# Gate columns of a hybrid decoder layer by Strassen's block product, seven products for eight

## The chip, the cores and the metric

The kernel runs on one core of a Trainium2 chip. The metric is the device time of one execution in microseconds (us). The core has a matrix engine (TensorE, PE in the rows), a vector engine (VectorE, DVE), a scalar engine (ScalarE, ACT), a general engine (GpSimd, POOL) and a queue engine (SyncE, SP), which here issues all transfers between DRAM and the on-chip memory. Each engine works through its own list of instructions in order and waits where an operand or a buffer is not there yet.

## The reference, cut to what matters

```python
h = rms_norm(x, norm_w)                       # x: 2048 tokens x 1024 channels
proj = h @ w_in                               # 8716 columns in all
(u_a, z_a, q, k, v, z_b, xbc, dt, z_c, gate_logits) = split(proj)
y_a = s5_mixer(u_a, ...) * silu(z_a)          # state space branch
y_b = attention_mixer(q, k, v, ...) * silu(z_b)
y_c = ssd_mixer(xbc, dt, z_c, ...)
gates = sigmoid(gate_logits)                  # 3 x 1024 columns: the gate columns
merged = gates_0*(y_a@proj_a) + gates_1*(y_b@proj_b) + gates_2*(y_c@proj_c)
return x + merged @ w_out
```

The change concerns the 3072 columns `gate_logits`, the last part of `h @ w_in`.

## The kernel before, in words

Everything is float32, and each operand of a large product is split in two numbers, hi and lo, that the matrix engine takes at its fast rate (`F32R`). A product is then three passes: hi by hi, hi by lo, lo by hi. The tokens are worked on in two halves of 1024, each of two blocks (`tb`) of 512. `hT[tb]` holds the normed input of a block, transposed: eight channel groups (`kt`) of 128 by 512 tokens, as hi and lo.

For each half the kernel goes through the columns of `w_in`: in the first half `main_qkv`, `main_dtz`, `main_xbc`, `main_uz`, `main_gates`; in the second `main_uz`, `main_qkv`, `main_dtz`, `main_xbc`, `main_gates`. These loops `yield` after each group of output columns (a step), and `run` puts pieces of other work between the steps by a table of step numbers: the attention, the tables and scans of the two state space branches (`s5`, `ssd`), the merge of the attention groups, and `out_weights`, which splits the later projection weights and stores them in DRAM (`pw_d`, `wo_d`). After both halves `final` forms the gated sum and the output projection. The order written there is a priority; the order in each engine's list is then fixed ahead of the run by a scheduler.

`main_gates` takes 12 units of 256 columns per half. For each unit it loads 1 MiB of raw weights (`wr`), ScalarE writes the hi part (`wh`, L368) and VectorE the lo part (`wl`, L369), and `ch_unit` (L392 to L394) forms four outputs of 128 columns by 512 tokens, each of 8 x 3 matmuls. ScalarE applies tanh (`e_g`, L571) and SP stores the result to `g_d`. The second half loads and splits the same weights anew.

A tile pool gives buffers by tag. `ev` has nine buffers of 128x512, shared by nearly everything that leaves an engine; `xb` has three; weights have a pool of their own, `wp`, with one `wr`, six `wh` and six `wl`.

## Time and profile before

| | |
|---|---|
| Time before, median of 3 runs (lowest to highest) | 2508.61 us (2507.28 to 2509.72) |
| The profiled execution, its time | 2515.92 us |
| Its span in the trace | 2513.9 us |
| Busy share of the span: PE, DVE, ACT, POOL | 97%, 53%, 31%, 28% |
| Mean granted clock of TensorE | 0.989 of full |
| Moved by DMA, mean rate | 453.41 MB, 180 GB/s |

The span is the time between the first and the last record of the profiled execution; its own time is 2 us longer, and 7.3 us above the median. Busy shares are sums over the whole span. A matmul's record covers its way through the array, so that records of neighbours overlap: the time that one takes from the next is the distance of their starts.

### The profile page before, as it was taken

To read this page: it belongs to the slowest core of one execution; us is meant where nothing else is said; L and a number is where in the kernel's file an instruction comes from. 1 tells how busy PE (TensorE), PEld (TensorE's weight loads), DVE (VectorE), ACT (ScalarE), POOL (GpSimd) and SP (SyncE) were. 2 spreads that over 40 slices of the span, in tenths; PEclk is the share of its full clock that TensorE was granted. 3 is DMA by queue.
4 is the path that set the end of the run, shared out by engine and by line. 5 is a ranking of instruction groups with operands and counts; after the bars stand their busy time and mean duration, and the time that the engine had idled before them with its cause. 6 is when DMAs were issued, how large, how long until landed. Compare 5 with 4: busy or idle time off the path is not lost.

```text
span 2513.9 us, 40157 instructions
## 1 busy us (share of the span) xinstructions
PE 2450.5 (97%) x15216; PEld 2155.8 (86%) x15216; DVE 1325.0 (53%) x2852; ACT 782.5 (31%) x1656; POOL 700.4 (28%) x737
## 2 busy tenths in 40 slices
PE   8999999999999999999999999999999899999999
PEld 8999988778888888899999988888888678888988
DVE  6963667853544333277765545632334767563321
ACT  4222235443443324222244244533332312121100
POOL 2262243501434430054342000000111455432120
PEclk8999999999999999999999999999999999999999
DMA  6443344447995336455554432433333688887986
GB/s 162 117 147 117 127 134 132 139 135 213 324 340 183 127 100 212 125 160 172 155 171 153 127 107 85 151 122 126 112 126 113 227 294 298 302 293 261 315 291 217
DMA packets 417088, 453.41 MB, mean 180 GB/s; under 512 B 103040, under 2 KB 358272, under 8 KB 409728
## 3 DMA queue, kind: packets, MB, share of 16 engines
q1 hardware_dynamic: 416896, 450.86, 56.2%
q8 instruction: 120, 1.97, 0.3%
q14 instruction: 72, 0.59, 0.1%
HBM read 304.80 MB, written 145.97 MB: 179 GB/s over the span
## 4 chain that ended last, share of the span: by engine, by line
PE 76%; DMA 8%; DVE 8%; POOL 4%; SPq 2%; issue 1%; ACT 1%; DVEq 0%; ACTq 0%; POOLq 0%
PE ps_g L392 6%; PE ps_g L394 6%; PE ps_g L393 6%; PE fp L1299 3%; PE fp L1301 3%; PE fp L1300 3%; PE ao L688 3%; PE ps_xbc L393 2%; PE ps_xbc L394 2%; PE ps_xbc L392 2%; PE ps_uz L394 2%; PE ps_uz L392 2%; PE ps_uz L393 2%; PE op L1332 2%; PE op L1330 2%; PE op L1331 2%
## 5 line engine op out<-in xcount | busy, mean ns | idle before, releaser
L392 PE MATMUL ps_g<-hT_hi,wh_g 128*128 128x512 f32 x768 | 308.4, 402 | 0.6 <-DVE e_uz L466 0.6
L394 PE MATMUL ps_g<-hT_hi,wl_g 128*128 128x512 f32 x768 | 306.4, 399 | 0.0
L393 PE MATMUL ps_g<-hT_lo,wh_g 128*128 128x512 f32 x768 | 305.7, 398 | 0.0
L813 POOL TENSOR_TENSOR sr<-tle,ahl 128x384 fp32r<-128x384 f32 x128 | 119.9, 960 | 447.3 <-PE sd L818 343.2
L392 PEld LDWEIGHTS ps_g<-hT_hi,wh_g 128*128 128x128 f32 x768 | 144.3, 188 | 33.3 <-DVE e_uz L466 1.3
L394 PEld LDWEIGHTS ps_g<-hT_hi,wl_g 128*128 128x128 f32 x768 | 144.5, 188 | 32.8
L393 PEld LDWEIGHTS ps_g<-hT_lo,wh_g 128*128 128x128 f32 x768 | 144.4, 188 | 32.4
L1299 PE MATMUL fp<-fy_hi,fp 128*128 128x512 f32 x384 | 153.9, 401 | 1.8 <-DMA fp<-pw_d 1.3
L1332 PE MATMUL op<-fo,fm_lo 128*128 128x256 f32 x512 | 146.6, 288 | 7.2 <-DVE fm_lo L1312 7.2
L1330 PE MATMUL op<-fo,fm_hi 128*128 128x256 f32 x512 | 148.0, 289 | 4.0 <-DMA fo<-wo_d 2.8
L1301 PE MATMUL fp<-fy_hi,fp 128*128 128x512 f32 x384 | 150.9, 393 | 0.0
L1300 PE MATMUL fp<-fy_lo,fp 128*128 128x512 f32 x384 | 150.3, 391 | 0.0
L1331 PE MATMUL op<-fo,fm_hi 128*128 128x256 f32 x512 | 146.3, 286 | 0.0
L1304 POOL TENSOR_TENSOR fm<-fm,fg 128x512 f32<-128x512 f32 x64 | 85.0, 1328 | 204.4 <-DVE fg L1302 193.7
L667 ACT ACTIVATE sm<-sm,ml 128x256 f32<-128x256 f32 (+1 forms) x192 | 86.4, 451 | 154.4 <-DVE ml L665 127.0
L392 PE MATMUL ps_xbc<-hT_hi,wh_xbc 128*128 128x512 f32 x320 | 129.7, 405 | 0.0
L394 PE MATMUL ps_xbc<-hT_hi,wl_xbc 128*128 128x512 f32 x320 | 129.4, 404 | 0.0
L393 PE MATMUL ps_xbc<-hT_lo,wh_xbc 128*128 128x512 f32 x320 | 129.1, 404 | 0.0
L369 DVE TENSOR_TENSOR wl_g<-wr_g,wh_g 128x512 fp32r<-128x512 f32 x96 | 75.1, 804 | 98.5 <-ACT wh_g L368 93.5
L506 DVE SCALAR_TENSOR_TENSOR ac_cv<-xb_cv,convw,ac_cv 128x512 f32<-128x512 f32 x120 | 101.3, 844 | 38.8 <-ACT ac_cv L504 38.5
L381 PE MATMUL ps_q<-wh_q,hT_hi 128*128 128x256 f32 x384 | 112.2, 293 | 2.1 <-ACT hT_hi L324 1.7
L382 PE MATMUL ps_q<-wl_q,hT_hi 128*128 128x256 f32 x384 | 110.8, 289 | 3.4 <-DVE wl_q L369 3.4
(418 smaller groups left out, 6922.7 us busy)
## 6 DMA issues: line engine op xcount, KB each, us to landing
fp<-pw_d SPq DMA_DIRECT2D x32, 1536.0 KB, 6.9
fo<-wo_d SPq DMA_DIRECT2D x16, 2048.0 KB, 8.7
wr_g<-in_w_in_dram SPq DMA_DIRECT2D x24, 1024.0 KB, 5.4
g_d<-e_g SPq DMA_DIRECT2D x96, 256.0 KB, 2.7
fg<-g_d SPq DMA_DIRECT2D x96, 256.0 KB, 7.4
pw_d<-owh SPq DMA_DIRECT2D x24, 512.0 KB, 7.1
wr_xbc<-in_w_in_dram SPq DMA_DIRECT2D x10, 1024.0 KB, 5.5
x<-in_x_dram SPq DMA_DIRECT2D x32, 256.0 KB, 5.4
```

What stands on the lines that cost most here:

```text
L381: nc.tensor.matmul(ps, hi[:, t], wh, start=kt == 0, stop=False)
L382: nc.tensor.matmul(ps, hi[:, t], wl, start=False, stop=False)
L392: nc.tensor.matmul(ps, wh, hi, start=kt == 0, stop=False)
L393: nc.tensor.matmul(ps, wh, lo, start=False, stop=False)
L394: nc.tensor.matmul(ps, wl, hi, start=False, stop=kt == KT - 1)
L813: nc.gpsimd.tensor_mul(r, self.tle.unsqueeze(1).to_broadcast([P, 3, P]), ahl[:, i, h0:h0 + 3].unsqueeze(2).to_broadcast([P, 3, P]))
L1299: nc.tensor.matmul(ps, W[k][0], yh[k], start=k == k0, stop=False)
L1300: nc.tensor.matmul(ps, W[k][0], yl[k], start=False, stop=False)
L1301: nc.tensor.matmul(ps, W[k][1], yh[k], start=False, stop=k == k1 - 1)
L1330: nc.tensor.matmul(ps, mh[k][:, t], W[k][0], start=k == 0, stop=False)
L1331: nc.tensor.matmul(ps, mh[k][:, t], W[k][1], start=False, stop=False)
L1332: nc.tensor.matmul(ps, mlo[k][:, t], W[k][0], start=False, stop=k == 7)
```

## The change

The gate columns of a unit are now formed as one product of two by two blocks. The rows of the block product are the two token blocks of a half, the inner index is the two halves of the eight channel groups (`kt` 0 to 3 and 4 to 7), and the columns are the two groups of 128 columns of the unit. Eight products of four channel groups (12 matmuls each) become seven, in Winograd's form of Strassen's scheme: four sums of token blocks (S1 to S4) and four of weight blocks (T1 to T4) go in, and the outputs are sums that are partly left in the PSUM bank where the next product adds to them (`x`, `z`, `w` in the code).

The token sums are made once per half by `sums` (S3 and S4 go through DRAM as `sum_d`, and `late_sums` fetches them when the gates begin; S4 then lies where the second block's first four channel groups lay). The weight operands of the seven products are made in the first half by `ops_made` (four raw pieces of 256 KiB, four differences on GpSimd, seven splits), and each is stored as 512 KiB in `gw_d`; in the second half `ops_read` loads the 84 operands from there and nothing is split. Operands go through a ring of five buffers (`sw`) and are asked for three products ahead. A copy of a bank that a later output needs is kept in an `ev` buffer by ScalarE (`keep`), and VectorE adds it to a bank before the tanh.

To make room, buffers move: the weight pool is closed and opened anew at five places (`room_for_sums` before the third unit of `main_uz` in the first half and before `main_xbc` in the second, the start and the end of `main_gates`), `out_weights` works in halves in `ev` buffers, the merge uses `xb` and `ev`, `xb` has four buffers, some buffers of the attention and the scan go from two or three to one or two, and the scan loads its next chunk at the end of a chunk. The attention of the second half is spread over steps 198 to 250 instead of 198 to 256, the scan of the first half starts at step 89 instead of 83, and `out_weights` at 92 instead of 88.

```diff
-ATTEND = 256
+ATTEND = 250
...
+    def room_for_sums(self, half):
+        self.close_left()
+        self.xq = self.left_pool(f"xq{half}")
+        self.wp = self.left_pool(f"wq{half}")
...
+            if half == 0 and u == 2:
+                self.room_for_sums(half)
...
+        if half:
+            self.room_for_sums(half)
...
+    def sums(self, half):
+        nc = self.nc
+        v, gp = nc.vector, nc.gpsimd
+        t0, t1 = self.hT[2 * half], self.hT[2 * half + 1]
+        self.S = {}
+        for i in (1, 2):
+            self.S[i] = tuple(self.xq.tile([P, 4, 512], F32R, name=f"S{i}_{half}_{x}") for x in ("hi", "lo"))
+        for k in range(4):
...
+                gp.tensor_add(a[nm], hi.bitcast(F32), lo.bitcast(F32))
+            s1, s2, s3, s4 = a["22"], self.ev(f"s2_{half}_{k}"), a["21"], a["12"]
...
+            for i, x in ((1, s1), (2, s2)):
+                self.split(x, self.S[i][0][:, k, :], self.S[i][1][:, k, :])
+            yield
+    def split(self, x, hi, lo):
+        self.nc.scalar.copy(hi, x)
+        self.nc.vector.tensor_sub(lo, x, hi.bitcast(F32))
...
+        for i, dst in ((1, t1[0:4]), (0, [tuple(q[:, k, :] for q in q3) for k in range(4)])):
+            for k in range(4):
+                e = self.ev(f"sl{half}_{i}_{k}")
+                nc.sync.dma_start(e, self.sum_d[i, k])
+                self.split(e, *dst[k])
...
+    def op_tile(self, name):
+        return self.wp.tile([P, 2, 4, P], F32R, name=name, tag="sw", bufs=5)
+    def ops_made(self, u):
...
+        for i, j in ((0, 0), (0, 1), (1, 1), (1, 0)):
+            t = self.gp.tile([P, 528], F32, name=f"gr{u}_{i}{j}", tag="xb", bufs=4)
...
+        def diff(i, a, b):
+            t = self.ev(f"gt{u}_{i}", (P, 4, P))
+            nc.gpsimd.tensor_sub(t, a, b)
+            return t
+        def put(p, x):
+            t = self.op_tile(f"gw{u}_{p}")
+            self.split(x, t[:, 0], t[:, 1])
+            nc.sync.dma_start(self.gw_d[u, p - 1], t.bitcast(F32).rearrange("p x k c -> p (x k c)"))
+            return t
+        yield 1, put(1, b11)
+        t1 = diff(1, b12, b11)
+        yield 5, put(5, t1)
...
+        t3 = diff(3, b22, b12)
+        t4 = diff(4, b21, t2)
+        yield 7, put(7, t3)
+        yield 4, put(4, t4)
+    def ops_read(self, u):
+        for p in (1, 5, 6, 3, 2, 7, 4):
+            t = self.op_tile(f"gw{u}_{p}")
+            self.nc.sync.dma_start(t.bitcast(F32).rearrange("p x k c -> p (x k c)"), self.gw_d[u, p - 1])
+            yield p, t
     def main_gates(self, half):
         nc = self.nc
...
+            order += [(u, p) for p in ((1, 5) if u < 11 else (1, 2, 5))]
+            if u:
+                order.append((u - 1, 4))
+            order += [(u, p) for p in ((6, 3, 2, 7) if u < 11 else (6, 3, 7, 4))]
-            wt = self.wtile(f"g{u}_{half}", [(C_G + u * 256, 256)])
...
+        weights(0, 1)
+        weights(0, 5)
+        self.late_sums(half)
+        t0, t1 = self.hT[tb[0]], self.hT[tb[1]]
+        opnd = {1: t0[0:4], 2: t0[4:8], 4: t1[4:8], 5: self.S[1], 6: self.S[2], 7: self.S[3], 3: self.S[4]}
...
+        for n, (u, p) in enumerate(order):
+            w = weights(u, p)
+            for x in order[n + 1:n + 4]:
+                weights(*x)
...
+            ps = bank["z"] if p in (5, 3) else bank["w"] if p == 2 else bank[u, "x"]
+            for k, (hi, lo) in enumerate(opnd[p]):
+                wh, wl = w[:, 0, k, :], w[:, 1, k, :]
+                nc.tensor.matmul(ps, wh, hi, start=k == 0 and p in (1, 2, 5), stop=False, skip_group_check=True)
+                nc.tensor.matmul(ps, wh, lo, start=False, stop=False, skip_group_check=True)
+                nc.tensor.matmul(ps, wl, hi, start=False, stop=k == 3 and p in (2, 3, 4), skip_group_check=True)
...
+            if u == 11 and p == 2:
+                if half:
+                    self.ysplit = [self.load_y(0)]
...
-                ps = self.mmps([P, 512], f"ps_{nm}")
-                self.ch_unit(wt, tb, m, ps)
-                e = self.ev(f"e_{nm}")
-                nc.scalar.activation(e, ps, AF.Tanh, scale=0.5)
...
+            for q in range(2):
+                raw = self.ev(f"ow{j}_{q}")
+                nc.sync.dma_start(raw, src[0, k * P:(k + 1) * P, q * 512:q * 512 + 512])
+                hl = [self.gp.tile([P, 512], F32R, name=f"ow{x}{j}_{q}", tag="ev", bufs=9) for x in "hl"]
...
-        run([(ssd0, 64, 83, 135), (early0, 8, 86, 122), (self.out_weights(), 20, 88, 134)], 136)
+        run([(self.sums(0), 4, 81, 87)], 88)
+        run([(ssd0, 64, 89, 135), (early0, 8, 90, 124), (self.out_weights(), 20, 92, 134)], 136)
```

How the lists of the engines differ, at three places. SP's list while the gates of the first half run: `gr` is a raw weight piece, `gw_d` the stored operands, `ow`, `pw_d`, `wo_d` belong to `out_weights`, `g_d` are results. Before, from the load of one unit's weights on:

```order
L353 DMA wr_g_0_8029<-in_w_in_dram 128x8x256 [waits DMAHW3_49,DVE_49]
L783 DMA sx_8127<-xs_d 128x768 [waits DMAHW4_49,PE_49,Pool_49]
L860 DMA yc_d<-sz_7363 128x6x128 [waits DMAHW5_49,Activation_49]
L1248 DMA wo_d<-owh_9062 128x4x256 [waits DMAHW6_49,Activation_49]
L1248 DMA wo_d<-owh_9062 128x4x256 [waits DMAHW7_49,DVE_49]
L1237 DMA ow_9316<-in_w_out_dram 128x1024 [waits DMAHW0_49]
L1248 DMA wo_d<-owh_9190 128x4x256 [waits DMAHW1_49,Activation_49]
L1248 DMA wo_d<-owh_9190 128x4x256 [waits DMAHW2_49,DVE_49]
L334 DMA hT_d<-xe_0_7727 128x4x128 [waits DMAHW3_49,Activation_49]
```

and after the change, within one unit:

```order
L1433 DMA pw_d<-owl_0_7870 128x4x128 [waits DMAHW4_49,DVE_49]
L649 DMA gw_d<-gw_6_7821 128x1024 [waits DVE_49]
L649 DMA gw_d<-gw_3_7883 128x1024 [waits DMAHW6_49,DVE_49]
L649 DMA gw_d<-gw_2_7902 128x1024 [waits DMAHW7_49,DVE_49]
L1433 DMA pw_d<-owh_1_7877 128x4x128 [waits DMAHW0_49,Activation_49]
L1433 DMA pw_d<-owl_1_7878 128x4x128 [waits DMAHW1_49,DVE_49]
L697 DMA g_d<-g_g_0_7918 128x512 [waits DMAHW2_49,Activation_49]
L638 DMA gr_01_7955<-in_w_in_dram 128x4x128 [waits DMAHW3_49,Pool_49]
L638 DMA gr_11_7957<-in_w_in_dram 128x4x128 [waits DMAHW4_49]
```

Between two results there are now stores of operands (128x1024 is 512 KiB) as well as the transfers of `out_weights`, which went further ahead before.

SP's list at the third unit of `main_uz` in the first half, the load of its raw weights with its neighbours, before:

```order
L469 DMA ua_d<-e_uz_1_0_6429 1024x1x64 [waits DMAHW5_49,Activation_49]
L469 DMA ua_d<-e_uz_0_1_6495 1024x1x64 [waits DMAHW6_49,Activation_49]
L353 DMA wr_uz_0_6890<-in_w_in_dram 128x8x256 [waits DMAHW7_49,DVE_49]
L691 DMA o_d_73<-ob_2_1_6332 128x264 [waits DMAHW0_49,DVE_49]
L1070 DMA p_d<-s5p_6539 128x512 [waits DMAHW1_49,Activation_49]
```

and after:

```order
L490 DMA ua_d<-e_uz_0_1_6861 1024x1x64 [waits Activation_49]
L372 DMA wr_uz_0_6900<-in_w_in_dram 128x8x256 [waits DMAHW3_49,PE_49]
L957 DMA sbt_7689<-bmT_d 128x2x128 [waits DMAHW5_49,DMAHW4_49,PE_49]
L490 DMA ua_d<-e_uz_1_1_6889 1024x1x64 [waits Activation_49]
L959 DMA sct_8100<-cmT_d 128x2x128 [waits DMAHW6_49]
L372 DMA wr_uz_0_7099<-in_w_in_dram 128x8x256 [waits DMAHW7_49,DMAHW3_49,DVE_49]
```

The load waited for VectorE, which reads the same buffer's former content when it splits; now it waits for PE, since the new pool's buffer lies where weights of the unit ahead lay, and it stands behind a result of that unit.

PE's list right there, before:

```order
L393 MATMUL ps_uz_1_1_6862<-hT_1_lo,wh_uz_0_3_6684 128x512
L394 MATMUL ps_uz_1_1_6862<-hT_1_hi,wl_uz_0_3_6685 128x512
L392 MATMUL ps_uz_0_0_6908<-hT_0_hi,wh_uz_0_0_6892 128x512 [waits PE_49]
L393 MATMUL ps_uz_0_0_6908<-hT_0_lo,wh_uz_0_0_6892 128x512
L394 MATMUL ps_uz_0_0_6908<-hT_0_hi,wl_uz_0_0_6893 128x512
L392 MATMUL ps_uz_0_0_6908<-hT_0_hi,wh_uz_0_0_6892 128x512
L393 MATMUL ps_uz_0_0_6908<-hT_0_lo,wh_uz_0_0_6892 128x512
```

and after:

```order
L1001 MATMUL sd_3_7442<-sr_3_0_7438,tgtr 128x384 [waits Pool_49]
L1001 MATMUL sd_3_7442<-sr_3_1_7440,tgtr 128x384 [waits Pool_49]
L411 MATMUL ps_uz_0_0_6918<-hT_0_hi,wh_uz_0_0_6902 128x512 [waits DMAHW1_49,PE_49,Activation_49]
L412 MATMUL ps_uz_0_0_6918<-hT_0_lo,wh_uz_0_0_6902 128x512
L411 MATMUL ps_uz_1_0_6971<-hT_0_hi,wh_uz_0_0_6902 128x512
L412 MATMUL ps_uz_1_0_6971<-hT_0_lo,wh_uz_0_0_6902 128x512
L411 MATMUL ps_uz_0_1_7020<-hT_0_hi,wh_uz_0_0_6902 128x512
L412 MATMUL ps_uz_0_1_7020<-hT_0_lo,wh_uz_0_0_6902 128x512
L413 MATMUL ps_uz_0_0_6918<-hT_0_hi,wl_uz_0_0_6903 128x512 [waits DVE_49]
```

Before, a bank was filled by its 24 matmuls one after the other right behind the former unit; now matmuls that need only the first split weights (`wh_uz_0_0`) are taken for three banks in turn.

## Rows read from the trace of the kernel before

**Rows 1.** The page, parts 1 and 2: busy time, and tenths in 40 slices.

```profile
PE 2450.5 (97%) x15216; PEld 2155.8 (86%) x15216; DVE 1325.0 (53%) x2852; ACT 782.5 (31%) x1656; POOL 700.4 (28%) x737
...
PE   8999999999999999999999999999999899999999
...
DMA  6443344447995336455554432433333688887986
```

**Rows 2.** Groups by line: the matmuls of the gates; busy, mean ns | idle before.

```profile
L392 PE MATMUL ps_g<-hT_hi,wh_g 128*128 128x512 f32 x768 | 308.4, 402 | 0.6 <-DVE e_uz L466 0.6
L394 PE MATMUL ps_g<-hT_hi,wl_g 128*128 128x512 f32 x768 | 306.4, 399 | 0.0
```

**Rows 3.** PE in order of time, 1707 to 1712 us: start us, us, what.

```profile
1707.18 0.39 PE L394 MATMUL ps_g<-hT_hi,wl_g 128*128 128x512 f32 x1
...
1711.82 0.40 PE L393 MATMUL ps_g<-hT_lo,wh_g 128*128 128x512 f32 x1
```

**Rows 4.** Windows: us; busy (x) of PE, PEld, DVE, ACT, POOL; clock; DMA share; GB/s.

```profile
640.00:974.00 334.00, 333.36 (x1597) 273.66 (x1596) 144.95 (x191) 118.39 (x230) 127.15 (x137) 1.00 0.64 205
1638.00:1986.00 348.00, 344.73 (x1821) 280.13 (x1819) 135.14 (x400) 114.02 (x314) 34.92 (x38) 1.00 0.39 125
...
1984.00:2513.00 529.00, 505.64 (x3009) 447.63 (x3007) 257.18 (x417) 77.12 (x146) 182.84 (x157) 0.98 0.83 286
```

**Rows 5.** Windows from 600 us on, columns as in rows 4.

```profile
600.00:620.00 20.00, 20.00 (x91) 16.36 (x91) 12.95 (x15) 8.81 (x13) 3.23 (x4) 1.00 1.11 335
620.00:640.00 20.00, 20.00 (x94) 16.40 (x93) 8.74 (x11) 7.55 (x11) 2.11 (x2) 1.00 1.08 314
700.00:720.00 20.00, 20.00 (x101) 16.70 (x100) 9.15 (x12) 9.14 (x18) 4.84 (x6) 1.00 1.08 374
...
600.00:760.00 160.00, 159.36 (x759) 130.97 (x759) 84.87 (x104) 69.60 (x123) 57.28 (x59) 1.00 1.05 331
```

**Rows 6.** Transfers by kind: KB of one, median us from issue to landing.

```profile
wr_g<-in_w_in_dram SPq DMA_DIRECT2D x24, 1024.0 KB, 5.4
g_d<-e_g SPq DMA_DIRECT2D x96, 256.0 KB, 2.7
...
pw_d<-owh SPq DMA_DIRECT2D x24, 512.0 KB, 7.1
...
wt_d<-s5w SPq DMA_DIRECT2D x16, 512.0 KB, 2.8
wr_uz<-in_w_in_dram SPq DMA_DIRECT2D x8, 1024.0 KB, 6.1
```

**Rows 7.** Groups by line on DVE, ACT and POOL: busy, mean ns | idle.

```profile
L369 DVE TENSOR_TENSOR wl_g<-wr_g,wh_g 128x512 fp32r<-128x512 f32 x96 | 75.1, 804 | 98.5 <-ACT wh_g L368 93.5 <-PE ps_g L393 4.6
...
L1302 DVE SCALAR_TENSOR_TENSOR fg<-fg,fp 128x512 f32<-128x512 f32 x64 | 43.1, 686 | 80.5 <-DMA fg<-g_d 74.2 <-PE fp L1301 5.6 <-PE ssp L839 0.5
...
L368 ACT CAST wh_g<-wr_g 128x512 fp32r<-128x512 f32 x96 | 57.1, 621 | 80.0 <-DMA wr_g<-in_w_in_dram 47.8 <-PE ps_g L393 29.2 <-PE ps_uz L393 2.0
L571 ACT ACTIVATE e_g<-ps_g 128x512 f32<-128x512 f32 x96 | 56.7, 598 | 173.5 <-PE ps_g L394 170.5 <-DMA kb<-k_d 1.7 <-issue 1.2
...
L1304 POOL TENSOR_TENSOR fm<-fm,fg 128x512 f32<-128x512 f32 x64 | 85.0, 1328 | 204.4 <-DVE fg L1302 193.7 <-DMA fy<-ya_d 5.6 <-DVE msc L712 3.6
```

**Rows 8.** Waits of PE: waited for, us in total, times, longest.

```profile
PE ap L676 <- ACT sm L667: 6.9, 5, 3.1
...
PE op L1330 <- DMA fo<-wo_d: 2.8, 2, 1.8
...
PE fp L1299 <- DMA fp<-pw_d: 1.3, 1, 1.3
```

**Rows 9.** Windows with idle PE: columns as in rows 4.

```profile
320.00:340.00 20.00, 16.81 (x123) 15.45 (x121) 13.84 (x29) 5.76 (x16) 8.72 (x8) 0.83 0.50 155
480.00:500.00 20.00, 17.29 (x99) 13.55 (x97) 17.88 (x32) 7.12 (x16) 14.28 (x13) 1.00 0.49 145
```

**Rows 10.** The split of gate weights on VectorE: duration ns min/median/max.

```profile
L369 DVE TENSOR_TENSOR wl_g<-wr_g,wh_g x96: 675/692/1850, 628.4 to 1957.2; 128x512 fp32r<-128x512 f32 x96
```

More of the change, by code (lines that the diff above doesn't have):

```diff
@@ new lines, in split, with late_sums @@
+    def split(self, x, hi, lo):
+        self.nc.scalar.copy(hi, x)
+        self.nc.vector.tensor_sub(lo, x, hi.bitcast(F32))
+    def late_sums(self, half):
+        nc = self.nc
+        t1 = self.hT[2 * half + 1]
+        q3 = tuple(self.wp.tile([P, 4, 512], F32R, name=f"S3_{half}_{x}") for x in ("hi", "lo"))
+        for i, dst in ((1, t1[0:4]), (0, [tuple(q[:, k, :] for q in q3) for k in range(4)])):
[3 more added lines that the diff above has]
+                self.split(e, *dst[k])
+            self.S[4 if i else 3] = dst
+        for i in (1, 2):
+            self.S[i] = [tuple(q[:, k, :] for q in self.S[i]) for k in range(4)]
@@ L555, in main_gates @@
+    def ops_read(self, u):
[3 more added lines that the diff above has]
+            yield p, t
     def main_gates(self, half):
         nc = self.nc
+        self.close_left()
+        self.wp = self.left_pool(f"wg{half}")
+        tb = (2 * half, 2 * half + 1)
+        order = []
         for u in range(12):
-            wt = self.wtile(f"g{u}_{half}", [(C_G + u * 256, 256)])
@@ new lines, in main_gates, with weights @@
+            if u:
+                order.append((u - 1, 4))
+            order += [(u, p) for p in ((6, 3, 2, 7) if u < 11 else (6, 3, 7, 4))]
+        gens = [(self.ops_read if half else self.ops_made)(u) for u in range(12)]
+        got = {}
+        def weights(u, p):
+            while (u, p) not in got:
+                q, t = next(gens[u])
+                got[u, q] = t
+            return got[u, p]
+        weights(0, 1)
+        weights(0, 5)
+        self.late_sums(half)
+        t0, t1 = self.hT[tb[0]], self.hT[tb[1]]
@@ L609, in fetch @@
             tag = "av" if what[0] == "v" else "aq"
-            t = self.h.ct(f"{what}{self.nm}", [P, 256], tag=tag, bufs=5 if tag == "av" else 4)
+            t = self.h.ct(f"{what}{self.nm}", [P, 256], tag=tag, bufs=4)
             self.nc.sync.dma_start(t, src[self.g].rearrange("(n i r) c -> n r i c", i=P, r=DIL[self.g])[i, self.r])
@@ L768, in ssd, with ssd_load, ssd_chunk @@
         nc = self.nc
+        got = self.ssd_load(half * 8)
         for ch in range(half * 8, half * 8 + 8):
-            yield from self.ssd_chunk(ch, slice((ch % 8) * 12, (ch % 8) * 12 + 12))
-    def ssd_chunk(self, ch, hs):
+            got = yield from self.ssd_chunk(ch, slice((ch % 8) * 12, (ch % 8) * 12 + 12), got)
+    def ssd_load(self, ch):
+        nc = self.nc
+        rows = slice(ch * P, (ch + 1) * P)
+        xs = self.sct(f"sx{ch}", [P, 768], tag="sx", bufs=2)
+        nc.sync.dma_start(xs, self.xs_d[rows])
+        bm = self.sct(f"sb{ch}", [P, 256], tag="sb", bufs=1)
+        nc.sync.dma_start(bm, self.bm_d[rows])
+        bT = self.sct(f"sbt{ch}", [P, 2, P], tag="sbt", bufs=1)
+        nc.sync.dma_start(bT, self.bmT_d[:, rows].rearrange("(g n) t -> n g t", n=P))
+        cT = self.sct(f"sct{ch}", [P, 2, P], tag="sct", bufs=2)
+        nc.sync.dma_start(cT, self.cmT_d[:, rows].rearrange("(g n) t -> n g t", n=P))
+        return xs, bm, bT, cT
+    def ssd_chunk(self, ch, hs, got):
         nc = self.nc
@@ L847, in ssd_chunk @@
             yield
+        nxt = self.ssd_load(ch + 1) if ch % 8 < 7 else None
         nc.vector.tensor_mul(y, y, z)
@@ L1415, in main @@
         st.close()
-        self.late = [None, None]
-        self.late[0], self.sp = open_pool("sp1")
         st, self.jp = open_pool("jp3")
-        ssd, merge = chain(self.ssd_dt(1, self.sp), self.ssd(1)), self.merge()
+        ssd, merge = self.ssd(1), self.merge()
         run([(chain(self.attention(0, 1), self.attention(1, 1), self.attention(2, 1)), 72, S5END + 2, ATTEND),
-             (early(ssd, 12), 12, 236, ATTEND)], ATTEND)
+             (self.sums(1), 4, 206, 222), (self.ssd_dt(1, self.jp), 2, 222, 232)], ATTEND)
         st.close()
-        self.late[1], self.mp = open_pool("mp")
-        run([(early(merge, 4), 4, ATTEND, 272), (early(ssd, 6), 6, ATTEND, 272)], 10 ** 6)
+        self.late, self.sp = open_pool("sp1")
+        run([(early(merge, 4), 4, ATTEND + 4, 272), (early(ssd, 16), 16, ATTEND, 272)], 10 ** 6)
         self.rest = [merge, ssd]
@@ L1438, in last @@
                     pass
-                self.late[1].close()
-                self.late[0].close()
+                self.late.close()
     def build(self):
@@ L1448, in build @@
             self.gp = ctx.enter_context(tc.tile_pool(name="gp", bufs=1))
[L1449 to L1450 removed]
+            self.left = []
+            self.wp = self.left_pool("wp")
+            self.main()
             self.fp = ctx.enter_context(tc.tile_pool(name="fp", bufs=1))
```

155 lines of the change are left out of this document (100 added, 55 removed).

## Prediction

> **What bounds the kernel now.** I read the page first. PE is busy in 97% of the span, at nine tenths in nearly every slice, the other engines in half of it or less [rows 1]. So a matmul that is taken out shortens the run, unless something else then sets the pace. What one is worth is not its record: the groups by line give 0.40 us for a matmul of the gates [rows 2], but these records overlap. In order of time, 21 neighbours with nothing between them start from 1707.18 to 1711.82 us, 20 steps in 4.64 us, 0.232 us each [rows 3].
>
> Then the windows of the two gate stages. In the first half (640 to 974 us) PE is busy 333.4 of 334 us; VectorE, ScalarE and GpSimd are at 145, 118 and 127 us; DMA moves 205 GB/s. In the second half (1638 to 1986 us) it is 344.7 of 348 us at only 125 GB/s [rows 4]. No wait of PE for a transfer is worth more than 2.8 us in all [rows 8]. The windows from 600 us on show the one thing that is near its limit: from 600 to 760 us, while `out_weights` runs, the DMA engines are busy 1.05 of their time (packets overlap) and move 331 GB/s, in the best slice 374 [rows 5]. PE does not suffer, as all of that is needed much later.
>
> **The change part by part.** *Matmuls.* Before: 12 units x 2 halves x 4 outputs x 24 = 2304. After: 12 x 2 x 7 products x 12 = 2016. At 0.232 us [rows 3] the 288 that go are worth 66.8 us, 33.4 in each half. PE's own work in the first gate stage falls from 334 to 301 us, in the second from 348 to 315.
>
> *Transfers, second half.* 12 raw loads of 1 MiB go (12.6 MB), 84 operands of 512 KiB come (44.0 MB), and 2 MB of token sums. The stage moved 125 GB/s x 348 us = 43.5 MB; it will move 77 MB in 315 us, 244 GB/s. `final` moves 286 GB/s over 529 us [rows 4], with all PE waits for its weights together 4.1 us [rows 8]. An operand is asked for three products ahead, 3 x 12 x 0.232 = 8.4 us, and 1 MiB landed in 5.4 us [rows 6]. I take nothing for waits here (bound: 4 us as in `final`; if the cover goes, that is if landing takes over 8.4 us, each product waits the rest).
>
> *Transfers, first half.* The stage moved 205 GB/s x 334 us = 68.5 MB. The 84 stores add 44.0 MB, the sums about 2. `out_weights` moved 335 and 314 GB/s from 600 to 640 us already [rows 5], 13.0 MB in all; in the new order it starts with the gates and runs evenly through them (SP's list above), so I count 10 of the 13 MB into the stage. Sum: 125 MB. At the best rate seen, 374 GB/s, that takes 334 us; at the mean of the saturated stretch, 331 GB/s, 378 us; PE wants 301. The stores have rows of 4 KiB; `wt_d`, the nearest such store of the same size, lands in 2.8 us where `pw_d` with its 512-byte rows takes 7.1 [rows 6], so I take the better rate: **the first gate stage stays at 334 us and its 33.4 us are lost**. It can't run away into the background: an operand's buffer, one of five, is free only when its store has landed, so PE follows the DMA.
>
> What the Trainium skill says speaks against this price. Its page "DMA: Bandwidth & Descriptors", section Bandwidth, gives 425 GB/s for one core's large transfers with the other core of its pair idle; by that the 125 MB would take 294 us, an estimate, and PE would set the pace. This trace shows no slice above 374, and 1.05 to 1.11 of the engines' time at 314 to 374.
>
> *Engines, first half.* 36 more splits on VectorE at 0.804, 36 additions from a bank at 0.686, 8 late splits: 145 + 29 + 25 + 6 = 205 us. ScalarE: 36 more splits at 0.621, 36 copies at 0.598, 8 late splits: 118 + 22 + 22 + 5 = 167 us. GpSimd: 48 differences at 1.33 (the nearest row is its addition of the same size): 127 + 64 = 191 us [rows 4, 7]. All under 301 us, so nothing is charged. The 16 token additions on GpSimd (21 us per half) and 24 VectorE operations (19 us) run beside `main_uz` and `main_xbc`, where PE needs neither; late by up to 20 us they would hold up the second product.
>
> *Seams.* Reopened pools put new buffers where old ones are still read. At the third unit of `main_uz` the load now waits for PE, behind a result of the unit ahead. Landing 6.1 us [rows 6], one split 0.6 [rows 7], issue some 0.5; against it about half of the last group of 24 matmuls (2.8 us) still runs: 4.4 us of idle PE (bounds: 0 if the buffer is free early, 7.2). PE's list after the change fits, with three banks taken in turn. The same at `main_xbc` of the second half, with attention to fill: 4 us. At the start of the second half, where the first weights land on S1 and S2, 2 us, and 1 us at each start of the gates, where `late_sums` must be split within three products: 12 us in all (0 to 20).
>
> *The rest.* The attention of the second half gets 52 steps instead of 58, some of them shorter; PE waited 6.9 us in all on its exponentials [rows 8], so up to 5 us, taken as 0. The scan's fewer buffers and the merge in `xb` lie beside work that has slack; taken as 0, bound 5.
>
> Sum: 0 in the first half, -33.4 in the second, +12 for seams: -21.4 us. The profiled execution, 2515.92, becomes 2494.5; it lay 7.3 us above the median of the runs, so the median goes from 2508.6 to **2487**.
>
> **The rivals.** *1. DMA keeps up.* Both halves gain: -66.8 + 12 = -54.8, 2454 us. For it: DMA time is 0.64 of the stage now [rows 4], the stores have long rows, and no trace here shows where 4 KiB rows saturate. Against it: 125 MB in 301 us is 415 GB/s, 11% above the best slice. Chance 0.22.
>
> *2. The first half gets slower than now.* Place: the ring of raw pieces and operands in the first gate stage. GpSimd reads a piece, SP loads the next into its buffer behind queued stores, GpSimd subtracts, ScalarE and VectorE split, and only then can PE go on. If the DMA gives 331 GB/s under this mix, the stage takes 378 us: +44 - 33.4 + 12 = +23, 2531 us. It decides from 334 + 21 = 355 us on, 29.6 us per unit against 27.8 now, or 352 GB/s. For it: 331 is a mean over 160 us, 374 one slice [rows 5]; where PE idled 3.2 us in 20 the clock fell to 0.83 of full in the slice, though not with 2.7 us elsewhere [rows 9]. Against it: the longer rows. A chance of 0.23 for a loss or none.
>
> *3. VectorE and GpSimd in each other's way.* The split took 675 ns at best, 692 in the median and 1850 at worst [rows 10]: some are held up. If the two never ran at once, the first stage would need 205 + 191 = 396 us: +62 - 33.4 + 12 = +41, 2549 us. The Trainium skill's page "SBUF — State Buffer" calls the port pair that the two share an exclusive lock. The median against the best says that most splits are not held up, and the busy times here hold what waiting there was. Chance 0.05.
>
> **How the numbers follow.** The forecast has 0.50 (its own range 2477 to 2499: seams 0 to 20, first half within 10 us), rival 1 0.22, rival 2 0.23, rival 3 0.05. The range goes from 2453, rival 1 with seams of 11, to 2518: this leaves out the lower part of rival 1 (0.08) and the upper ones of 2 and 3 (0.12). This kernel can tell 0.2%, 5 us, from no change. Faster: 0.46 of the forecast and 0.21 of rival 1, 0.67. Same: 0.04 of the forecast, 0.01 of rival 1 and 0.08 of rival 2, 0.13. Slower: 0.20.
>
> **What would show it.** Right: 2016 gate matmuls still 0.232 us apart; a first gate stage of 325 to 345 us with DMA at 350 to 380 GB/s and its share at 1 or above; PE in that stage waiting for splits whose own wait is for a landing (raw piece or stored operand); a second stage of about 315 us at 240 GB/s; idle PE of 3 to 7 us at the third unit of `main_uz` and the first of `main_xbc`. Wrong: a first stage near 301 us (rival 1), one above 355 (rival 2, or 3 if DMA is below 330 GB/s and VectorE's splits are far over 0.8 us), waits of 1 us or more per product for operands in the second half, or a `final` that starts later behind scan and merge.

## Result, and the profile after the change

The changed kernel takes 2670.99 us (median of 4 runs, 2669.36 to 2671.5), the kernel before 2509.16 us in the same session: ratio 1.0643, 95% interval 1.0625 to 1.0662. It is slower by about 160 us, where 22 us faster was forecast; no rival reached that far.

The page of the changed kernel, parts 1 and 2 (busy time; tenths in 40 slices), answers to [rows 1]:

```profile
span 2669.5 us, 40705 instructions
PE 2466.6 (92%) x14928; PEld 2143.8 (80%) x14928; DVE 1433.1 (54%) x3028; ACT 838.1 (31%) x1768; POOL 821.4 (31%) x817
...
PE   8999999998877788899999999999988998998999
...
PEclk9999999999888888899999999999988999998999
DMA  6453444535878888736655432367756887877886
```

There are 288 matmuls fewer, as planned, and yet PE is busy for 16 us more, in a span that is 156 us longer. The digits say where: slices 10 to 16, the first gate stage, are at 7 and 8, and the granted clock falls there too. Before, PE stood at 9 in nearly every slice [rows 1].

The stages, from the windows of the changed kernel (columns as in rows 4): first gate stage, the stretch between the two gate stages, second gate stage, `final`.

```profile
642.00:1086.00 444.00, 349.34 (x1460) 272.85 (x1460) 226.72 (x299) 172.85 (x337) 200.84 (x184) 0.88 0.83 276
1086.00:1770.00 684.00, 664.91 (x4603) 609.25 (x4604) 413.82 (x788) 248.62 (x497) 159.54 (x188) 0.99 0.48 144
1770.00:2120.00 350.00, 325.41 (x1627) 260.42 (x1626) 136.70 (x393) 115.82 (x308) 42.86 (x41) 0.94 0.72 233
2118.00:2670.00 552.00, 516.15 (x3011) 450.59 (x3009) 241.38 (x444) 74.15 (x139) 175.42 (x157) 0.96 0.79 271
```

Read to the microsecond from windows of 1 us, the 155.6 us of span divide so: the first gate product starts 3 us later; the first gate stage takes 443 us instead of 334 (+109); from its end to the first gate product of the second half, 685 instead of 665 (+20); the second stage 349 instead of 347 (+2, where -33 was forecast); from the last gate product to the end 550.5 instead of 528.9 (+22).

In the first gate stage no engine and no queue is full: VectorE 227 of 444 us, GpSimd 201, ScalarE 173, the DMA engines 0.83 of their time at 276 GB/s. That is the picture of a chain of waits, not of a bound. The waits of PE in this stage (waited for, us in total, times, longest):

```profile
PE xT L300 <- DVE x L294: 26.7, 8, 8.2
PE psx_g L717 <- ACT gw L609: 22.1, 5, 8.7
PE psz_g L717 <- ACT gw L609: 16.1, 4, 5.0
PE syd L1010 <- DVE sm L1004: 15.4, 7, 3.0
PE psz_g L717 <- ACT gz L701: 7.0, 3, 4.7
```

PE waits for operands that ScalarE splits (`gw`, 38 us), but no less for the norm of the second half's tokens (the transposes `xT`, made by `a0_early`) and for the scan (`syd`), 42 us together, whose arithmetic the change left alone. So look at what ScalarE waited for in the same stretch:

```profile
ACT owh L1425 <- DMA ow<-in_w_out_dram: 43.7, 9, 9.3
ACT xj L288 <- DMA x<-in_x_dram: 35.8, 13, 7.2
...
ACT owh L1425 <- DMA ow<-in_proj_c_dram: 19.4, 5, 6.5
...
ACT owh L1425 <- DMA ow<-in_proj_a_dram: 14.3, 5, 3.9
```

In these rows ScalarE stands 113 us before loads of `out_weights` (77) and of the norm (36). The same view of the kernel before has `out_weights` with 12.7 us:

```profile
ACT owh L1239 <- DMA ow<-in_w_out_dram: 7.9, 3, 3.9
...
ACT owh L1239 <- DMA ow<-in_proj_c_dram: 4.8, 2, 3.7
```

An engine takes its list in order, so all casts, copies out of PSUM and activations behind such a wait are late as well, and PE with them. An idle PE then costs a second time. In order of time (start, length), PE of the changed kernel after one such wait, and the windows around it:

```profile
810.05 0.50 PE L717 MATMUL psz_g<-hT_hi,gw 128*128 128x512 f32 x1 [2.02 <-ACT gz L701]
...
812.42 0.63 PE L718 MATMUL psz_g<-hT_lo,gw 128*128 128x512 f32 x1
812.85 0.63 PE L719 MATMUL psz_g<-hT_hi,gw 128*128 128x512 f32 x1
```

```profile
806.00:811.00 5.00, 2.98 (x13) 2.13 (x12) 3.39 (x5) 3.00 (x6) 1.91 (x3) 1.00 1.02 383
811.00:814.00 3.00, 3.00 (x9) 2.35 (x8) 2.74 (x3) 1.14 (x2) 2.03 (x2) 0.50 1.04 306
```

PE had been idle for 2 of the 5 us before; then its clock is 0.50, the lower of its two levels (1.2 GHz), and the starts are 0.43 us apart instead of 0.232. Over the whole stage the sum is 444 us = 95 us of idle PE and 349 us of busy PE. The experiment f6 below (no stores, `out_weights` with its own load buffers) has the same work in this stage but for the norm, and there PE is busy 300 us at a clock of 0.99; the norm's 64 transposes took 8.3 us in the stage of the kernel before:

```profile
L295 PE MATMUL xT<-ident,x 128*128 128x128 f32 x64 | 8.3, 272 | 0.0
```

So 95 us are waits, some 41 us (an estimate, 349 less 308) the lower clock that follows them, and 308 us the work itself, for which the prediction had 301.

### The profile page after: what moved, and what is told of

The parts are those of the page before. It is cut to its first block, busy times and chain, and to the rows that moved or that the text cites. A ratio compares the mean times of both kernels' runs of the same rounds, so it can differ in the third digit from the quotient of the medians.

```text
span 2669.5 us, 40705 instructions
## 1 busy us (share of the span) xinstructions
PE 2466.6 (92%) x14928; PEld 2143.8 (80%) x14928; DVE 1433.1 (54%) x3028; ACT 838.1 (31%) x1768; POOL 821.4 (31%) x817
## 4 chain that ended last, share of the span: by engine, by line
PE 47%; DMA 10%; DVE 5%; POOL 2%; SPq 2%; ACT 2%; issue 2%; DVEq 0%; ACTq 0%; POOLq 0%
PE fp L1485 3%; PE fp L1487 3%; PE fp L1486 3%; PE op L1516 2%; PE psx_g L717 2%; PE op L1517 2%; PE op L1518 2%; PE psx_g L718 2%; PE psx_g L719 2%; DMA fg<-g_d 2%; PE ao L859 2%; PE ps_xbc L413 1%; PE ps_xbc L411 1%; PE ps_xbc L412 1%; PE ps_uz L411 1%
## 5 line engine op out<-in xcount | busy, mean ns | idle before, releaser
L1485 PE MATMUL fp<-fy_hi,fp 128*128 128x512 f32 x384 | 157.1, 410 | 18.2 <-ACT fy_hi L1457 9.4
L1487 PE MATMUL fp<-fy_hi,fp 128*128 128x512 f32 x384 | 154.4, 402 | 0.0
L411 PE MATMUL ps_uz<-hT_hi,wh_uz 128*128 128x512 f32 x256 | 103.7, 405 | 12.3 <-ACT wh_uz L387 12.3
L402 PE MATMUL ps_q<-wh_q,hT_lo 128*128 128x256 f32 x384 | 109.6, 286 | 2.5 <-DVE hT_lo L330 2.4
L400 PE MATMUL ps_k<-wh_k,hT_hi 128*128 128x256 f32 x384 | 109.8, 288 | 0.0
L401 PE MATMUL ps_k<-wl_k,hT_hi 128*128 128x256 f32 x384 | 108.5, 284 | 1.0 <-DVE wl_k L388 1.0
L400 PE MATMUL ps_v<-wh_v,hT_hi 128*128 128x256 f32 x384 | 109.3, 286 | 0.0
L402 PE MATMUL ps_k<-wh_k,hT_lo 128*128 128x256 f32 x384 | 108.6, 284 | 0.0
L402 PE MATMUL ps_v<-wh_v,hT_lo 128*128 128x256 f32 x384 | 108.0, 282 | 0.0
```

Of the source, the lines that this page charges most:

```text
L400: nc.tensor.matmul(ps, hi[:, t], wh, start=kt == 0, stop=False)
L401: nc.tensor.matmul(ps, hi[:, t], wl, start=False, stop=False)
L402: nc.tensor.matmul(ps, lo[:, t], wh, start=False, stop=kt == KT - 1)
L411: nc.tensor.matmul(ps, wh, hi, start=kt == 0, stop=False)
L1485: nc.tensor.matmul(ps, W[k][0], yh[k], start=k == k0, stop=False)
L1487: nc.tensor.matmul(ps, W[k][1], yh[k], start=False, stop=k == k1 - 1)
```

## Experiments

Two theories stood at the start. **Queues:** buffers that the change put into shared rings make loads late, engines wait in order, and PE starves. **DMA** (rival 2 of the prediction): the 44 MB of stores fill the transfer engines. All times in one table, read from windows of 1 us; the runs that are named by letter follow below. The last column counts from the last gate product to the end of the span; the expectations, written earlier, count `final` from its first product (514 us before, 552 changed) and take the changed kernel's first gate stage as 440 or 456 us, not 443. Each run but the changed kernel (4 executions), f7 (12) and g3 (10) is a single execution; the kernel before, executed beside them, went from 2503 to 2518 us, so a few us between two single runs mean nothing by themselves.

| run | first gate stage | second gate stage | behind it | run, us |
|---|---|---|---|---|
| before | 334 | 347 | 529 | 2509 |
| changed kernel | 443 | 349 | 550 | 2671 |
| e1_nostore | 399 | 360 | 565 | 2652 |
| e2_ow_later | 355 | 348 | 550 | 2632 |
| e3_plain_both | 379 | 365 | 561 | 2655 |
| e4_half2_made | 379 | 363 | 542 | 2626 |
| b1_ow_ring | 361 | 347 | 522 | 2532 |
| b3_ssd_bufs | 336 | 358 | 529 | 2521 |
| b4_merge_ssd | 338 | 359 | 557 | 2553 |
| f1_own_raw | 400 | 348 | 544 | 2626 |
| s1_nostore_ow | 333 | 360 | 549 | 2613 |
| f4_raw_mp_att | 395 | 332 | 528 | 2593 |
| f5_raw_mp_att_a0 | 339 | 334 | 530 | 2555 |
| f6_f5_nostore | 308 | 341 | 527 | 2523 |
| f8_stored | 339 | 328 | 519 | 2531 |
| f7_both_made | 310 | 335 | 520 | 2511 |
| g1_second_only | 335 | 341 | 529 | 2516 |
| g2_merge_late | 335 | 338 | 529 | 2512 |
| g3_ssd_own | 336 | 338 | 521 | 2506 |

**e1, the stores taken away.** The second half makes its operands again, in four buffers, and the first four merge tiles get buffers of their own.

```diff
             self.split(x, t[:, 0], t[:, 1])
-            nc.sync.dma_start(self.gw_d[u, p - 1], ...)
...
-        gens = [(self.ops_read if half else self.ops_made)(u) for u in range(12)]
+        gens = [self.ops_made(u, half) for u in range(12)]
```

> All 84 stores of operands in the first half are gone (44 MB of the stage's 127 MB); the second half makes its operands again from raw pieces, with four operand buffers there, and the first four merge tiles have buffers of their own. If the DMA engines pace the first gate stage (rival 2): 83 MB at the 278 GB/s of the changed kernel take 298 us, so the stage falls from 456 to 300-335 us and the run to 2515-2550 us. If the in-order queues pace it (making an operand waits on GpSimd, ScalarE and VectorE behind out_weights, the norm and the scan): the stage stays at 410-455 us, and the run is 2620-2680 us.

399 us, just under the range of the queue theory, and far from the 300 to 335 of DMA. With 198 GB/s and a DMA share of 0.66 it is still 65 us longer than before. The stores cost 44 us on top of something larger.

**e2, `out_weights` elsewhere.**

```diff
-        run([(ssd0, 64, 89, 135), (early0, 8, 90, 124), (self.out_weights(), 20, 92, 134)], 136)
+        run([(ssd0, 64, 89, 135), (early0, 8, 90, 124)], 136)
...
-        run([(self.s5(), 42, 153, 180)], 180)
+        run([(self.s5(), 42, 153, 180), (self.out_weights(), 20, 138, 178)], 180)
```

> out_weights runs beside S5 in the second half instead of in the first gate stage; all else as in the changed kernel. ScalarE's waits for its pieces (77 us) leave the stage, and 31 MB of transfers. Queue theory: the stage falls from 456 to 340-390 us with PE at full clock for most of it, DMA well under 0.9; the run 2570-2610 us. Rival 2 (DMA at 278 GB/s): 95 MB, 343 us, with the DMA share still at 0.83 or above. If the norm's transposes and the scan are the cause: 430 us or more.

The stage falls by 88 us to 355, with a DMA share of 0.75: the queue theory. More than half of it is lost again beside S5, where the stretch to the second gates takes 734 us instead of 685; the run gains 39 us, less than expected.

**e3, the room without Strassen.** `main_gates` of the kernel before stands in the changed kernel's pools, buffers and order; the token sums are left out.

```diff
+        if half in (0, 1):
+            yield from self.plain_gates(half)
+            return
...
-        run([(self.sums(0), 4, 81, 87)], 88)
+        run([], 88)
...
-             (self.sums(1), 4, 206, 222), (self.ssd_dt(1, self.jp), 2, 222, 232)], ATTEND)
+             (self.ssd_dt(1, self.jp), 2, 222, 232)], ATTEND)
```

> The changed kernel's pools, buffers and order, but the gates of both halves as plain products of 24 matmuls (2304 in all), without token sums and operands. It prices the room alone. If the room made for Strassen costs only what the prediction put down (seams, at most 12-20 us): 2515-2530 us, the first gate stage 334-345 us. If out_weights and the norm in the ring of nine are what starves the stage: the first gate stage above 380 us here too, the run above 2560 us.

2655 us: **the room alone costs 146 us**, before a single product is saved. It shows the loop at work. In order of time, first SP (issues), then ScalarE:

```profile
716.15 0.45 SPq L1453 DMA_DIRECT2D ow<-in_proj_a_dram  x1
...
720.42 0.37 SPq L1463 DMA_DIRECT2D pw_d<-owh  x1
720.85 0.49 SPq L1453 DMA_DIRECT2D ow<-in_proj_a_dram  x1
```

```profile
719.76 0.63 ACT L1455 ACTIVATE owh<-ow 128x512 fp32r<-128x512 f32 x1 [2.37 <-DMA ow<-in_proj_a_dram]
724.35 0.63 ACT L1455 ACTIVATE owh<-ow 128x512 fp32r<-128x512 f32 x1 [3.96 <-DMA ow<-in_proj_a_dram]
724.89 1.07 ACT L687 ACTIVATE e_g<-ps_g 128x512 f32<-128x512 f32 x2
```

A half piece is loaded at 716.15, cast at 719.76, and only then is the next load issued, at 720.85, to be cast at 724.35. Each half piece, of which there are 40, takes 4.6 to 4.7 us. ScalarE stands in that time, here for 2.4 and 4.0 us, and the gates' results (`e_g`) wait behind it. No load runs ahead, as each of three tiles per half piece needs one of nine buffers that the gates, the norm and the scan go through as well.

**e4, Strassen in the second half only, on that room.** As e3 in the first half, as e1 in the second.

> First half plain (1152 matmuls), second half seven products with operands made there, nothing stored or read back; first four merge tiles in buffers of their own. Queue theory: the second half has GpSimd, ScalarE and VectorE nearly free and no out_weights or norm, so making them costs PE little: second gate stage 315-330 us (348 before, 356 in the changed kernel), the run 30 us below the kernel with plain gates in both halves. If making operands is too slow by itself (VectorE and GpSimd in each other's way, rival 3): 380 us or more.

2626 us, 30 below the plain version, as expected; but the second stage took 363 us, not 315 to 330. The trace shows why: from 1925 to 1969 us the last attention blocks, the first merge tile and the start of the scan ran on PE one after the other, with a single gate product (12 matmuls) among them and one idle time of 9.5 us. The changed kernel has the same hole (windows, columns as above):

```profile
1980.00:2000.00 20.00, 16.48 (x83) 11.90 (x82) 9.27 (x38) 6.74 (x28) 0.00 (x0) 0.63 0.24 74
2000.00:2020.00 20.00, 8.11 (x25) 6.09 (x24) 11.07 (x27) 2.04 (x5) 11.30 (x11) 0.59 0.56 182
```

**b1, b3, b4, parts of the room put into the kernel before, alone.**

```diff
-            raw = self.ct(f"ow{j}", [P, D], tag="ow", bufs=2)
-            hl = self.ct(f"owh{j}", [P, 2, D], F32R, tag="owh", bufs=2)
+                raw = self.ev(f"ow{j}_{q}")
+                hl = [self.gp.tile([P, 512], F32R, name=f"ow{x}{j}_{q}", tag="ev", bufs=9) for x in "hl"]
```

> The kernel before with one part of the change alone: out_weights in halves, its raw piece and both results in the ring of nine. No Strassen, no other buffer changed. Ring theory (a piece's load can be issued only when an old buffer of the ring is free, and ScalarE waits for it in order, with the gates' weights and results behind): the first gate stage, 335 us before, takes 360-385 us and the run 2535-2565 us. If the stall in the plain version came from the seams and the shifted order instead: stage 335-345 us, run 2510-2520 us.

361 us, at the low end of the range, the run 23 us longer, just under its own: `out_weights` in the ring, raw pieces and results, is a cost by itself, with no Strassen near it. For b3 the functions `ssd`, `ssd_load` and `ssd_chunk` of the changed kernel were taken over, for b4 also its `merge`.

> The kernel before with the scan of the changed kernel alone (one buffer for B, its transpose and z, the next chunk's loads ahead, the product with the state in the ring of nine). If the scan's buffers cost `final` its extra 40 us: final 535-555 us (514 before), run 2530-2555 us. If they are as free as the prediction had it: 2508-2516 us.

> As the kernel with the scan alone, and the merge in the rings of four and nine too. If the merge in the rings is what slows `final`: final 545-560 us and 20 us or more above the scan alone; if the scan is: within 8 us of the scan alone; if neither: 2508-2518 us, and final's loss lies in the later start of both.

The scan's buffers cost 12 us, but not in `final`: the second gate stage grows by 11 us, where PE waited 10.8 us once for the first merge tile. The merge in the rings costs 28 us behind the gates (557 against 529). Its waits of PE, and then of SP's queue:

```profile
PE fp L1313 <- DMA fp<-pw_d: 13.7, 3, 9.4
PE fp L1313 <- ACT fy_hi L1285: 7.8, 1, 7.8
```

```profile
SPq L1350 <- DVE my L724: 20.3, 7, 5.0
SPq L704 <- DMA out_dram<-ox: 14.7, 7, 6.5
```

L704 loads a merge tile into `xb` and waits for a result of `final` (`ox`) to leave that ring; L1350 loads `ox` and waits for the merge (`my`). The two hold each other up in SP's list, and the weights `pw_d` are issued behind them: before, PE waited 1.3 us for these [rows 8], here 13.7.

**f1, f4, f5, the repairs one after the other, on the changed kernel.**

```diff
-                raw = self.ev(f"ow{j}_{q}")
+                raw = self.owp.tile([P, 512], F32, name=f"ow{j}_{q}", tag="ow", bufs=2)
```

> The changed kernel with one thing put back: out_weights' raw pieces (2 KB a partition) get two buffers of their own, outside the ring; its results stay in it. Ring theory, loads late: a piece is there when ScalarE comes to it, the first gate stage falls from 440 to 385-410 us and the run to 2615-2645 us. If the results that wait for their stores hold the ring: 430-440 us, run 2660-2675 us.

Two buffers of 2 KB a partition, and the run is 45 us shorter; loads now run ahead (ScalarE waits 7.9 us for them in the stage). ScalarE's largest wait is then the norm's `x`, 31.1 us.

```diff
+                ta, tz = (self.mp.tile([P, 528], F32, name=f"mo{x}{tt}", tag=f"mo{x}", bufs=2) for x in "ab")
...
-        run([(chain(self.attention(0, 1), ...), 72, S5END + 2, ATTEND),
+        run([(chain(self.attention(0, 1), ...), 72, S5END + 2, ATTEND - 5),
```

> The changed kernel with three things put right: out_weights' raw pieces in two buffers of their own (as measured, 395 us for the first gate stage); the merge from its fifth tile on in a pool of its own that opens after the gates; the attention of the second half ends five rows earlier, so that gate products run beside its last blocks. If the merge in the rings costs `final` its 40 us: final 515-525 us. If the hole in the second gate stage is the tail of attention with nothing beside it: that stage 320-330 us. Run 2565-2590 us; were neither the cause, 2620 us.

Both causes are seen, each smaller than expected, and the run ends 3 us above its range: 16 us behind the gates for the merge's own pool, 16 us in the second gate stage for the attention's end, of which the stretch before it, with 59 more of the attention's matmuls, takes 3 back.

```diff
-        run([(ssd0, 64, 89, 135), (early0, 8, 90, 124), (self.out_weights(), 20, 92, 134)], 136)
+        run([(ssd0, 64, 89, 135), (self.out_weights(), 20, 92, 134)], 136)
...
+             (self.ssd_dt(0, self.jp), 3, 73, 79), (early0, 8, 42, 76)], 80)
```

> The same, and the norm of the second half's tokens (a0_early) moved ahead of the gates, beside the attention of the first half. PE waited 27 to 33 us for its tiles in the first gate stage. If these waits are its own: the stage falls by 25-40 us more, run 2530-2560 us. If the next thing in the queues takes their place: less than 10 us.

56 us less in the first stage (395 to 339), more than the 27 to 33 us of waits that it takes away; but the gates begin 16 us later, as the norm's work now stands ahead of them, so the run gains 38.

**s1 and f6, the stores again.** s1 is e1 and e2 together; f6 is f5 without the stores.

> The changed kernel with out_weights moved beside S5 and without the 84 stores (operands made in both halves). It asks what making the operands costs by itself in the first gate stage (355 us with out_weights moved and the stores kept, 400 us without stores and out_weights in place). If the two losses are separate: 315-335 us. If PE still waits on the chain GpSimd, ScalarE, VectorE and on the norm's transposes: 340-355 us, so that there is no gain from fewer matmuls in this half, even then.

> The repaired version (own raw buffers, merge's pool, attention's end, the norm ahead of the gates; 336 us and 338 GB/s in the first gate stage) without the 84 stores; the second half makes its operands. If the stage is paced by DMA, as the prediction had it (125 MB, 334 us): with 44 MB less TensorE sets the pace, 305-318 us. If making the operands paces it: 328-338 us.

s1: 333 us, inside the first range. f6: 308 us, inside the first range too. The windows of the stage with and without the stores (f5, f6):

```profile
661.00:1000.00 339.00, 309.88 (x1396) 246.07 (x1396) 219.16 (x275) 152.80 (x288) 198.79 (x168) 0.96 0.98 337
```

```profile
657.00:965.00 308.00, 300.02 (x1396) 240.18 (x1396) 236.72 (x275) 150.98 (x288) 208.10 (x168) 0.99 0.74 227
```

The stage of f4, with the norm still in it:

```profile
645.00:1040.00 395.00, 333.99 (x1460) 265.81 (x1460) 232.42 (x299) 173.16 (x337) 205.75 (x184) 0.91 0.91 310
```

With the queues put right the stores set the pace: a DMA share of 0.98 at 337 GB/s and 339 us; without them PE is busy 300 of 308 us. Making the operands is no bound: VectorE 237 and GpSimd 208 of 308 us.

**g1, g2, g3, Strassen in the second half alone.** The first half is that of the kernel before; operands are made, not read back.

> First half as in the kernel before (plain gates, out_weights with its own buffers, the scan with two buffers), Strassen in the second half alone with operands made there, merge and attention's end as in the version with three repairs. If the loss was all in the room and the queues of the first half, final and the attention's tail: first gate stage 335 us, second 315-325 us (345 before), final 515-525 us, run 2480-2500 us, below the kernel before. If making operands or the seam at the first xbc unit eats the 33 us: 2505-2530 us.

> Strassen in the second half alone (2516 us), with the first four merge tiles four rows later. TensorE stood 8 us at the first one's transposes in that version. If that wait is latency after the last attention block: 6-10 us less, 2506-2511 us. If the wait only moves: 2514-2518 us.

> The same, and the scan from its eleventh chunk on has two buffers for B and its transpose and one of its own for z and for the product with the state, in the pool that opens after the gates. If the scan's single buffers and its use of the ring are what is left in `final` (530 us against 514): 515-522 us, run 2495-2505 us. If it is the merge or the later start of both: 525-530 us, run as without it.

2516, 2512 and 2506 us. The merge's shift gave 4 us, between its two readings, and the scan's own buffers 6 us, both less than single runs spread. The stages say a little more: 3 us in the second gate stage for the shift, 8 behind the gates for the buffers; counted from its first product `final` was still 530 us (that product now starts before the last of the gates), so that the single buffers are a part of what is left there and not all. g3 against before: ratio 0.9988, interval 0.9975 to 1.0001.

**f7, f8, both halves with all repairs.** f7 makes the operands twice, f8 stores and reads them.

> Both halves Strassen, operands made in each, with all repairs: own raw buffers of out_weights, the norm ahead of the gates, attention's end earlier, merge and the late scan in a pool after the gates, merge four rows later. From 2523 us: 10 us less in `final` (as the scan's buffers gave) and 4 in the second gate stage: 2507-2512 us. If the seams were smaller than the gain of 27 us in the first stage: 2490-2505 us.

> The same with the operands stored in the first half and read back in the second. Against making them twice the first gate stage is 336 instead of 308 us, the second about the same or 5 us shorter: 2530-2545 us. If reading back frees the second half by more than storing costs: below 2515 us.

f7: 2511 us, ratio 1.0006 (0.9993 to 1.0018). f8: 2531 us. Storing costs 29 us in the first gate stage (339 against 310) and reading back saves 7 in the second (328 against 335). No version beats the kernel before by more than can be measured. Where f7's 66.8 us of matmuls went can be read only from its profiled execution, which lay 7 us below its median while that of the kernel before lay 7 above: the spans differ by 11 us, the medians by 2 the other way. PE is busy 46 us less than before and idle 98 us instead of 63:

```profile
PE 2404.2 (96%) x14928; PEld 2101.0 (84%) x14928; DVE 1534.6 (61%) x3112; ACT 880.0 (35%) x1852; POOL 907.7 (36%) x865
```

The two gate stages are 24 and 12 us shorter than before and the rest behind them 9, but the gates begin 12 us later and the stretch between the stages is 21 us longer. Much of this is work that has moved: the norm's 64 transposes now stand ahead of the gates, and 104 matmuls of the attention have gone from the second gate stage (540 before, 436 now) into the stretch. The stretch before, and in f7:

```profile
974.00:1638.00 664.00, 650.32 (x4550) 597.06 (x4548) 388.59 (x754) 242.39 (x478) 140.11 (x175) 1.00 0.49 147
```

```profile
961.00:1647.00 686.00, 667.43 (x4662) 610.82 (x4662) 412.49 (x799) 252.75 (x513) 158.83 (x186) 0.99 0.48 143
```

So 17 of the 21 us are busy time of PE, and 5 are waits.

## Why the prediction was wrong

**What was right, and what was luck.** Matmuls still start 0.232 us apart at full clock, and PE's need of 301 us shows as 300 in f6, or 308 with the norm's transposes. The stage's traffic, 125 MB forecast, was 123 (276 GB/s for 444 us). That the stores would set the pace was right once the queues are repaired (f5, f8: a share of 0.97 to 0.98). That they then give 339 us, with 334 forecast, is partly luck, as two errors cancel. The rate is 335 to 337 GB/s and not the 374 of the best slice, and the stage of f5 moves only 114 MB (337 GB/s for 339 us), since the norm has left it. At 337 GB/s the 125 MB would take 371 us, an estimate; f4, with the norm in the stage, took 395 us at 310 GB/s. The mean of the saturated stretch, 331 GB/s and 378 us, which the prediction left to rival 2, was the better price. In the second half 244 GB/s and waits of at most 4 us were forecast; the trace has 233 GB/s and, from 1700 to 2000 us, 4.4 us of PE's waits for stored operands.

The page "DMA: Bandwidth & Descriptors" of the Trainium skill, section Bandwidth, would have had PE set the pace with its 425 GB/s. No stage here shows that rate: where the share was 0.98, it was 337, so the measurement decides for the lower price.

**The step that failed first: "Engines, first half ... All under 301 us, so nothing is charged".** Busy times were added up and compared with the stage, and what makes room in it was put at nothing; 334 us were forecast and 443 measured. None of the engines off PE was busy for more than 227 of 444 us, and still the stage was lost to waiting. What should have been priced is the change of `out_weights`: one line in the list of what makes room, its buffers counted by nobody. It lost its own buffers, two for raw pieces and two for results, and got tiles from a ring whose other users had grown. In the changed kernel moving it away, with its own transfers and casts, shortens the stage by 88 us, and giving its loads two buffers back by 43 (e2, f1). That the change of `out_weights` alone, raw pieces and results, costs the kernel before 27 us in that stage was shown too (b1). The norm, which the change moved by four steps only, is the second part: 56 us of the stage, 38 of the run (f5). Its loads sit in the same ring and its transposes in PE's list; but f5 takes its work out of the stage as well, so that the ring is the reason is argued here and not shown by itself. With f1, f4 and f5 together the stage is back at 339 us.

The Trainium skill has the rule in one line ("Trainium Kernel Development and Optimization", section Best Practices: double-buffer, to overlap transfers with compute). This trace agrees: 77 us of ScalarE's waits for `out_weights`' loads where they share the ring, 12.7 before with two buffers of their own, 7.9 in f1.

**"The scan's fewer buffers and the merge ... taken as 0, bound 5".** Measured in the kernel before: 28 us behind the gates for the merge, 11 us in the second gate stage for the scan (b3, b4). Both are beyond the bound. Slack of an engine is no slack of a ring: `final`'s own loads share it.

**"The attention ... up to 5 us, taken as 0".** Ending it five steps earlier gave 16 us in the stage, 13 with the stretch before it (f4): its last blocks, which wait on each other, had no product beside them.

**Seams, 12 us (0 to 20).** Right in the sum. In the changed kernel PE waited for the third unit of `main_uz` (4.4 us forecast), for the first weights of the second half (2) and for those of `main_xbc` (4):

```profile
PE ps_uz L411 <- ACT wh_uz L387: 6.4, 1, 6.4
```

```profile
PE ps_uz L411 <- ACT wh_uz L387: 6.0, 1, 6.0
...
PE ps_xbc L411 <- ACT wh_xbc L387: 1.9, 1, 1.9
```

With 1.6 us at the first start of the gates this is 16 us. What the sum left out is that the attention's 52 steps move work: of the 20 us by which the stretch between the gate stages grew, 15 are busy time of PE (664.9 against 650.3 us), with 45 matmuls of the attention that stood in the second gate stage before.

**The second half's -33.4** came as +2 in the changed kernel, and as 12 to 19 us once the tail of the attention was repaired (f7 335, f4 332, f8 328), 315 being forecast; a part of this gain is attention that has moved ahead of the stage. What the rest is I did not divide: in f8 PE is busy 313 of the 328 us, at a mean granted clock of 0.97, where the kernel before has 1.00.

**The rivals.** Rival 2 named the right place, a ring in the first gate stage, and the falling clock; but it took the ring of raw pieces and operands, let the DMA's rate set its price, and ended at 378 us for the stage. Rival 3 is out as the pace: with 237 us on VectorE and 208 on GpSimd the stage ran in 308 us (f6). VectorE's splits did take longer there, 1.04 to 1.06 us in the mean where 0.804 was taken, which is a part of why it was busy 237 us and not 205; no run shows whether GpSimd is the reason.

```profile
L609 DVE TENSOR_TENSOR gw<-gt,gw 128x512 fp32r<-128x512 f32 x48 | 50.1, 1057 | 14.4 <-ACT gw L608 13.9
```

What none of them held is a part of the kernel that isn't in the change's arithmetic at all. Not followed up: e1 needs 15 us more behind its gates than the changed kernel.

## What to carry to other kernels

When a change needs room, price the room first, by itself: here the plain product in the new room (e3) was already 146 us slower, and the changed kernel 162. For each buffer that moves into a shared ring, count the ring's allocations per unit of time against the time a tile is held; when a load can no longer run ahead, every instruction behind its first reader waits, and busy shares don't show it. And a product saved on the bound engine is worth only what the waits leave: with all repairs PE was busy 46 us less in the profiled execution and idle 35 us more. Before a stage's gain is counted, see which work has moved out of it: a part of the 36 us that f7's gate stages gained stands again ahead of them and between them.

## What was not expected of the hardware

The waits cost some four tenths again: with PE's 95 us of idle time in the first gate stage came some 41 us (an estimate, above) of slower matmuls, at a mean granted clock of 0.88 (0.99 in f6). After a stretch of 5 us with 2 us idle it ran at the lower level for 3 us, with starts 0.43 us apart.
